# Loading stored operands of an fp32 transformer trunk into the tile of their low part, with no staging buffer between

## The chip, the cores and the metric

The kernel runs on one core of one Trainium2 chip, in one launch. The metric is the time of the whole program on the device, in microseconds (us).

## The reference

The program is a trunk of two layers over 1,024 tokens of width 1,024, in float32. Layer 0 mixes tokens by forgetting attention (FoX, 8 heads), layer 1 by chunkwise retention (4 heads); each is followed by a SwiGLU FFN of inner width 2,816, and a last RMSNorm ends it.

```python
def swiglu(h, w_in, w_out):
    gu = h @ w_in
    return (jax.nn.silu(gu[..., :D_FF]) * gu[..., D_FF:]) @ w_out

def reference(x, ...):
    for i in range(DEPTH):
        h = rmsnorm(x, norm_mix[i])
        j = i // N_MIXERS
        if i % N_MIXERS == 0:
            x = x + forgetting_attention(h, fox_w_in[j], fox_b_f[j], fox_w_out[j])
        else:
            x = x + retention(h, ret_w_in[j], ret_w_out[j])
        h = rmsnorm(x, norm_ffn[i])
        x = x + swiglu(h, ffn_w_in[i], ffn_w_out[i])
    return rmsnorm(x, final_norm)
```

Retention projects q, k, v and a gate g from the normed input, rotates q and k, sums `(q k) v` under a decay of the head, norms the result over 512 values of a head, multiplies by `silu(g)` and projects back.

## The kernel before

**High and low parts.** Every float32 operand of a product is split in two fp32r tiles of 128x512: `hi` is the value rounded (a copy by ScalarE, line 98), `lo` is the rest (a subtraction by VectorE, line 99). A product is three matmuls: `hi.hi`, `hi.lo`, `lo.hi`. A pair of such tiles is made by `units(pool)`; the pools are `bpa` with 32 tiles and `bpb` with 24. Weights have their own pool `wp` with tags `wh` and `wl`, 6 tiles each.

**Products.** The large projections (`Products`, lines 617 to 656) multiply blocks of two by two in seven products rather than eight. Each of the seven takes one weight block (A11, S1, S2, A12, S3, A22, S4) and one operand (B11, T1, T2, B21, T3, T4, B22); an operand is four pairs of tiles, one for each of four row blocks. `open` makes the first product, `middle` the next four, `close` the last two. `in_turn` and `paired_out` run many of these one after another, and open the next before they close the current one, except at the end of `in_turn` and, in `paired_out`, for the last of the four column blocks (`n == 3`). Copies by ScalarE free a PSUM bank for the next product: line 666, 683 or 687 behind S3, line 642 behind A11.

**What is kept in memory.** The FFN's inner activations do not fit on the chip. 16 of the 22 blocks are written to memory as the seven operands of two groups (`Stored.put`, tensors `ac0_0_...` to `ac1_1_...`, shown in the profile as ac_T and ac_B) and read back by `Stored.get` when a product of `paired_out` first wants them; the other six are written as they are (`ad`) and read back by `load_units`. In retention the rotated q and k (`qd`, `kd`), the values (`vd`), the gates (`gd`) and the normed results (`zd`) go through memory too. `prepare(h)` brings in one head: `load_k` (k, split, and also transposed by TensorE and scaled into tiles at lines 1034 and 1035), `load_units` for q, `load_v` for the values. `scores(h, ...)` makes `q k` for the next stage while `weighted` multiplies the values in the current one; `state(h)` sums `k v` for the second half of a head.

**Staging.** All of these reads, and the weights of both kinds of projection (`Blocks`, `wtile2`), first land in tiles of tag `st`, 128x1024, of which there are five. A tile of `st` is free again when the splits that read it are done. The half-megabyte loads of `Stored.get` and `load_units` are issued by SP.

**Order.** The order of each engine's instructions is set when the program is built, by a scheduler that goes by the order of the code and by its own estimate of what is ready. On the chip each engine then works its list in order, and waits where something is not there yet.

Of the kernel before, what the change touches and what calls it, by code (L numbers as in the profile page):

```python
# [10 lines left out]
F32 = mybir.dt.float32  # L11
F32R = mybir.dt.float32r
AF = mybir.ActivationFunctionType
ALU = mybir.AluOpType
# [3 lines left out]
P = 128  # L18
# [3 lines left out]
H = 512  # L22
# [15 lines left out]
def trunk(ctx, tc, nc, d, out):  # L38
# [16 lines left out]
    def nm(s):  # L55
        cnt[0] += 1
        return f"{s}_{cnt[0]}"
# [18 lines left out]
    def units(pool):  # L76
        return [pool.tile([P, H], F32R, tag="b", name=nm("b")) for _ in range(2)]
# [19 lines left out]
    def split(hi, lo, src):  # L97
        nc.scalar.copy(hi, src)  # L98
        return nc.vector.tensor_tensor(lo, src, hi.bitcast(F32), op=ALU.subtract)  # L99
# [10 lines left out]
    HALF = (slice(0, H), slice(H, S))  # L110
# [74 lines left out]
    with ExitStack() as fs:  # L185
# [52 lines left out]
        def v_pair(p, rc):  # L238
            ws = []
            wid = VF0 if p == 0 else 256  # L240
            src = d["fox_v0"] if p == 0 else d["fox_v"][p - 1]
            for k in range(0, KT, 2):
                hi, lo = wload(src[:, k * wid:(k + 2) * wid], 2 * wid)
                ws += [(hi[:, j * wid:(j + 1) * wid], lo[:, j * wid:(j + 1) * wid]) for j in range(2)]
            vs = []
            z = small([P, TB, FOX_HEADS], "fz", 1) if p == 0 else None
            for b in range(TB):
                if p == 0 and b in (3, 4):
                    ps = mp.tile([P, H], F32, tag="st", name=nm("mm"), bufs=2)
                else:  # L250
                    ps = mm_fox()
                tk = slice(b % 4 * P, (b % 4 + 1) * P)
                for k in range(KT):
                    xh, xl = xg[k][b // 4]
                    wh, wl = ws[k]
                    nc.tensor.matmul(ps[:, :wid], xh[:, tk], wh, start=(k == 0), stop=False)  # L256
                    nc.tensor.matmul(ps[:, :wid], xh[:, tk], wl, start=False, stop=False)  # L257
                    nc.tensor.matmul(ps[:, :wid], xl[:, tk], wh, start=False, stop=(k == KT - 1))  # L258
                vh = fp.tile([P, 256], F32R, tag="vh", name=nm("vh"), bufs=12)
                vl = fp.tile([P, 256], F32R, tag="vl", name=nm("vl"), bufs=12)  # L260
                r = rc[:, b:b + 1]
                nc.scalar.activation(vh, ps[:, :256], AF.Copy, scale=r)
                nc.vector.scalar_tensor_tensor(vl, ps[:, :256], r, vh.bitcast(F32), op0=ALU.mult, op1=ALU.subtract)
                if p == 0:
                    nc.vector.scalar_tensor_tensor(z[:, b, :], ps[:, 256:VF0], r, bf, op0=ALU.mult, op1=ALU.add)
                vs.append((vh, vl))
            return vs, z
# [150 lines left out]
        for h in range(2):  # L418
            ks.append([fp.tile([P, S], F32R, tag=t, name=nm(t)) for t in ("kh", "kl")])
            for b in range(2):  # L420
                tag, n = (("mm", 3), ("mm", 3), ("st", 2), ("st", 2))[2 * h + b]
# [20 lines left out]
        vs, z = v_pair(0, rc)  # L442
# [22 lines left out]
        for i, (n, b) in enumerate(TILES):  # L465
            if i < 3:
                mm_u(ops[n, b], wo[n][6:], last_o[:1], b, first=False, last=(i < EVAC))
            else:
                if n == len(wo):
                    wo.append(wtile(d["fox_o"][n][:, :7 * P], 7))  # L470
                tag, bufs = TAGS[i]
# [12 lines left out]
    bpb = ctx.enter_context(tc.tile_pool(name="bpb", bufs=24))  # L484
    yq = ctx.enter_context(tc.tile_pool(name="yq", bufs=4))
    sp = ctx.enter_context(tc.tile_pool(name="sp", bufs=1))
# [4 lines left out]
    def bsplit(pool, src):  # L491
        hi, lo = units(pool)
        split(hi, lo, src)
        return hi, lo


    NAMES = ("B11", "T2", "T1", "T3", "B21", "B22", "T4")
    MAP1 = dict(zip(NAMES, (bpb, bpb, bpb, bpa, bpa, bpa, bpa)))
# [3 lines left out]
    class Combos:  # L502
# [32 lines left out]
        def get(self, n):  # L535
            return self.t[n]

    class Stored:
# [15 lines left out]

        def get(self, n):
            if n not in self.t:
                self.t[n] = []
                for i in range(2):
                    st = sp.tile([P, 1024], F32, tag="st", name=nm("st"), bufs=5)
                    nc.sync.dma_start(st, self.d[n][:, i * 1024:(i + 1) * 1024])  # L560
                    self.t[n] += [bsplit(self.pools[n], st[:, HALF[j]]) for j in range(2)]
            return self.t[n]

    def wsplit(src):
# [213 lines left out]

    def load_units(pool, src, gate=None):

        r = []
        st = sp.tile([P, 1024], F32, tag="st", name=nm("st"), bufs=5)
        nc.sync.dma_start(st, src)
        if gate is not None:
            gt = sp.tile([P, 1024], F32, tag="st", name=nm("st"), bufs=5)
            nc.sync.dma_start(gt, gate)
            nc.vector.tensor_tensor(st, st, gt, op=ALU.mult)
        for h in range(2):
            r.append(bsplit(pool, st[:, HALF[h]]))
        return r  # L790

    def out_proj(wsrc, y, acts, xnew, gi, nextw, pools):
# [21 lines left out]
    def ffn(i, X, nrm, xold, xnew, last, nw, pools):  # L814
# [26 lines left out]
        y = paired_out(d["ffn_out_pairs"][i], stored, True, xold)  # L841
        wsrc = d["ffn_out"][i]
        acts = [load_units(bpa if last else bpb, t) for t in ad]
        if not last:
            return out_proj(wsrc, y, acts, xnew, 2, d["ret_qk"][1], MAP2)
# [157 lines left out]
    nc.sync.dma_start(mask, d["ret_mask"])  # L1003

    def load_v(h, b):
        st = sp.tile([P, 1024], F32, tag="st", name=nm("st"), bufs=5)[:, :512]
        nc.sync.dma_start(st, vd[b][:, h * 512:(h + 1) * 512])
        m = vmean[h][:, b:b + 1]
        hi, lo = units(bpb)
        nc.scalar.activation(hi, st, AF.Identity, bias=m)  # L1010
        nc.vector.scalar_tensor_tensor(lo, st, m, hi.bitcast(F32), op0=ALU.add, op1=ALU.subtract)
        return hi, lo
# [46 lines left out]
    def prepare(h):  # L1059
        kk, kt = load_k(h)  # L1060
        qq = [load_units(bpa, qd[h][e]) for e in range(2)]
        vv = [load_v(h, b) for b in range(TB)]
        heads[h] = [kk, kt, qq, vv, None, []]
# [102 lines left out]
    zg = list(zip(zd, [None] * (4 * 1) + gd[4 * 1:]))  # L1166
    y = [[None, None] for _ in range(KT)]
    acts = [load_units(bpa, *t) for t in zg[:8]]
    for n in range(KT):
        w = wtile2(d["ret_o"][n], 8)  # L1170
# [103 lines left out]
```

## Time and profile before

| | us |
|---|---|
| median of 3 runs | 2590.07 (2589.15 to 2590.61) |
| time of the profiled execution | 2592.81 |
| its span, first to last instruction | 2591.0 |
| TensorE busy (matmuls) | 2562.7 (99%) |
| VectorE busy | 1838.6 (71%) |
| ScalarE busy | 1229.5 (47%) |

The profile is of one execution. An engine's busy time is the time in which it had an instruction under way; matmuls overlap at their ends, so a busy TensorE is not one at its peak. The mean granted TensorE clock of the execution is 0.997 of full speed, and DMA moved 312 MB, 120 GB/s over the span.

The first FFN runs from about 520 to 1130 us of the span, retention's heads from about 1580 to 1785 us, the second FFN from about 1940 us to the end.

### The profile page before, as it was taken

What the parts mean: (1) busy time and instruction counts of PE and PEld (TensorE: products, weight loads), DVE (VectorE), ACT (ScalarE), POOL (GpSimd) and SP (SyncE); (2) the same over time, 40 slices, a digit from 0 to 9 for tenths busy, and PEclk for the clock granted to TensorE, in tenths of its full rate; (3) what the DMA queues carried; (4) which work ended last, traced back from release to release, by engine and by line L of the source; (5) the groups of instructions that cost most, each with busy time, mean ns of one, the idle gap of its engine ahead of it and who ended that gap; (6) DMA issues with size and microseconds to landing.
All of it is one profiled execution on the core that took longest, in us unless ns stands there. A gap on an engine that the chain in (4) does not pass through costs nothing.

```text
span 2591.0 us, 35137 instructions
## 1 busy us (share of the span) xinstructions
PE 2562.7 (99%) x12808; PEld 2184.6 (84%) x12808; DVE 1838.6 (71%) x3131; ACT 1229.5 (47%) x2320; POOL 169.5 (7%) x147
## 2 busy tenths in 40 slices
PE   9999999999999999999999999999999999999998
PEld 8889887888888888889898989898888888888788
DVE  6798888866666768886656576885567666667784
ACT  6566666543333454554343435762354333335543
POOL 0143323000000000001001010000000000000000
PEclk9999999999999999999999999999999999999999
DMA  3111142432332345533332334555522332325441
GB/s 131 44 58 65 51 146 96 149 106 95 113 106 98 127 147 182 161 115 124 102 107 98 122 103 154 191 194 195 195 87 94 105 107 94 110 89 179 167 147 66
DMA packets 137695, 312.12 MB, mean 120 GB/s; under 512 B 15665, under 2 KB 28721, under 8 KB 137521
## 3 DMA queue, kind: packets, MB, share of 16 engines
q1 hardware_dynamic: 136800, 309.33, 35.4%
q8 instruction: 100, 1.64, 0.3%
q14 instruction: 75, 0.61, 0.1%
q10 hardware_dynamic: 720, 0.55, 0.1%
HBM read 217.54 MB, written 92.27 MB: 120 GB/s over the span
## 4 chain that ended last, share of the span: by engine, by line
PE 93%; DVE 2%; issue 1%; DMA 1%; ACT 1%; POOL 0%; DVEq 0%; SPq 0%; POOLq 0%; ACTq 0%
PE mm L635 18%; PE mm L636 18%; PE mm L637 18%; PE mm L106 7%; PE mm L107 7%; PE mm L108 7%; PE mm L751 2%; PE mm L749 2%; PE mm L750 2%; PE mm L256 1%; PE mm L257 1%; PE mm L258 1%; DMA st<-ac_T 1%; PE mm L1101 1%; PE mm L1102 1%
## 5 line engine op out<-in xcount | busy, mean ns | idle before, releaser
L635 PE MATMUL mm<-b,wh 128*128 128x512 f32 x2128 | 827.6, 390 | 5.3 <-ACT 22_4491_22622 L683 3.5
L636 PE MATMUL mm<-b,wh 128*128 128x512 f32 x2128 | 829.3, 390 | 0.0
L637 PE MATMUL mm<-b,wl 128*128 128x512 f32 x2128 | 825.9, 390 | 0.0
L98 ACT CAST wh<-st 128x512 fp32r<-128x512 f32 (+1 forms) x449 | 276.4, 617 | 521.7 <-PE mm L636 318.6
L635 PEld LDWEIGHTS mm<-b,wh 128*128 128x128 f32 x2128 | 400.0, 188 | 88.6 <-ACT 22_4491_22622 L683 4.0
L637 PEld LDWEIGHTS mm<-b,wl 128*128 128x128 f32 x2128 | 400.0, 188 | 83.1
L636 PEld LDWEIGHTS mm<-b,wh 128*128 128x128 f32 x2128 | 400.1, 188 | 82.0
L99 DVE TENSOR_TENSOR wl<-st,wh 128x512 fp32r<-128x512 f32 (+1 forms) x449 | 317.7, 711 | 189.6 <-ACT wh L98 186.1
L98 ACT CAST wh<-s 128x512 fp32r<-128x512 f32 x252 | 156.5, 622 | 306.9 <-PE mm L636 272.9
L106 PE MATMUL mm<-b,wh 128*128 128x512 f32 x736 | 286.5, 392 | 7.7 <-ACT b L126 5.4
L107 PE MATMUL mm<-b,wh 128*128 128x512 f32 x736 | 287.4, 391 | 1.7 <-DVE b L99 1.7
L108 PE MATMUL mm<-b,wl 128*128 128x512 f32 x736 | 287.5, 391 | 0.0
L99 DVE TENSOR_TENSOR wl<-s,wh 128x512 fp32r<-128x512 f32 x252 | 179.8, 715 | 93.3 <-ACT wh L98 89.2
L106 PEld LDWEIGHTS mm<-b,wh 128*128 128x128 f32 x736 | 138.7, 189 | 37.1 <-ACT b L126 6.1
L107 PEld LDWEIGHTS mm<-b,wh 128*128 128x128 f32 x736 | 138.7, 188 | 29.5 <-DVE b L99 2.2
L99 DVE TENSOR_TENSOR b<-st,b 128x512 fp32r<-128x512 f32 x216 | 140.7, 675 | 31.4 <-ACT b L98 28.9
L98 ACT CAST b<-st 128x512 fp32r<-128x512 f32 x216 | 124.5, 611 | 80.9 <-DMA st<-ac_T 26.5
L108 PEld LDWEIGHTS mm<-b,wl 128*128 128x128 f32 x736 | 138.7, 188 | 28.1
L750 PE MATMUL mm<-wl,b 128*128 128x256 f32 x448 | 126.6, 283 | 0.0
L749 PE MATMUL mm<-wh,b 128*128 128x256 f32 x448 | 126.3, 283 | 0.0
L751 PE MATMUL mm<-wh,b 128*128 128x256 f32 x448 | 126.3, 283 | 0.0
L588 DVE TENSOR_TENSOR s<-st 128x512 f32<-128x512 f32 x84 | 58.3, 694 | 65.8 <-DMA st<-ffn_in 27.8
(498 smaller groups left out, 3891.2 us busy)
## 6 DMA issues: line engine op xcount, KB each, us to landing
st<-ffn_in SPq DMA_DIRECT2D x88, 512.0 KB, 3.5
st<-ffn_out_pairs SPq DMA_DIRECT2D x32, 512.0 KB, 4.1
st<-ac_T SPq DMA_DIRECT2D x32, 512.0 KB, 4.8
ac_T<-t SPq DMA_DIRECT2D x48, 256.0 KB, 2.4
st<-ac_B SPq DMA_DIRECT2D x24, 512.0 KB, 4.0
st<-fox_qk SPq DMA_DIRECT2D x32, 256.0 KB, 2.7
xo<-xd SPq DMA_DIRECT2D x32, 256.0 KB, 3.0
ac_B<-t SPq DMA_DIRECT2D x32, 256.0 KB, 2.4
```

The costliest lines, as they stand in the source:

```text
L98: nc.scalar.copy(hi, src)
L99: return nc.vector.tensor_tensor(lo, src, hi.bitcast(F32), op=ALU.subtract)
L106: nc.tensor.matmul(ps, wh, xh, start=(first and k == 0), stop=False)
L107: nc.tensor.matmul(ps, wh, xl, start=False, stop=False)
L108: nc.tensor.matmul(ps, wl, xh, start=False, stop=(last and k == n - 1))
L588: nc.vector.tensor_tensor(self.s1, self.a21, self.a22, op=ALU.add)
L635: nc.tensor.matmul(ps, hi[:, js], th, start=first and j == 0, stop=False, skip_group_check=True)
L636: nc.tensor.matmul(ps, hi[:, js], tl, start=False, stop=False, skip_group_check=True)
L637: nc.tensor.matmul(ps, lo[:, js], th, start=False, stop=(j == 3), skip_group_check=True)
L749: nc.tensor.matmul(o, th[:, tk], hi[:, js], start=f, stop=False, skip_group_check=True)
L750: nc.tensor.matmul(o, th[:, tk], lo[:, js], start=False, stop=False, skip_group_check=True)
L751: nc.tensor.matmul(o, tl[:, tk], hi[:, js], start=False, stop=(j == 3), skip_group_check=True)
```

## The change

`landed(pool, src)` is new: it takes a pair of tiles from the pool, has the DMA write the float32 data straight into the `lo` tile, and splits it there, so that `lo` is both source and destination of the subtraction. `Stored.get` uses it with four loads of a quarter-megabyte in place of two of half a megabyte; `load_units` uses it when there is no gate, with two loads in place of one. With a gate, the gate is still loaded into an `st` tile, the operand lands in `lo`, the product is written over the gate, and is split from there. `load_v` also lands in `lo`. `load_k`, the weights and the first loads of attention are as before, and `st` still has five tiles.

```diff
+    def landed(pool, src):
+
+        hi, lo = units(pool)
+        nc.sync.dma_start(lo.bitcast(F32), src)
+        split(hi, lo, lo.bitcast(F32))
+        return hi, lo
+
@@ Stored
         def get(self, n):
             if n not in self.t:
-                self.t[n] = []
-                for i in range(2):
-                    st = sp.tile([P, 1024], F32, tag="st", name=nm("st"), bufs=5)
-                    nc.sync.dma_start(st, self.d[n][:, i * 1024:(i + 1) * 1024])
-                    self.t[n] += [bsplit(self.pools[n], st[:, HALF[j]]) for j in range(2)]
+                self.t[n] = [landed(self.pools[n], self.d[n][:, j * H:(j + 1) * H]) for j in range(4)]
             return self.t[n]
@@ load_units
+        if gate is None:
+            return [landed(pool, src[:, HALF[h]]) for h in range(2)]
         r = []
-        st = sp.tile([P, 1024], F32, tag="st", name=nm("st"), bufs=5)
-        nc.sync.dma_start(st, src)
-        if gate is not None:
-            gt = sp.tile([P, 1024], F32, tag="st", name=nm("st"), bufs=5)
-            nc.sync.dma_start(gt, gate)
-            nc.vector.tensor_tensor(st, st, gt, op=ALU.mult)
+        gt = sp.tile([P, 1024], F32, tag="st", name=nm("st"), bufs=5)
+        nc.sync.dma_start(gt, gate)
         for h in range(2):
-            r.append(bsplit(pool, st[:, HALF[h]]))
+            hi, lo = units(pool)
+            z = gt[:, HALF[h]]
+            nc.sync.dma_start(lo.bitcast(F32), src[:, HALF[h]])
+            nc.vector.tensor_tensor(z, lo.bitcast(F32), z, op=ALU.mult)
+            split(hi, lo, z)
+            r.append((hi, lo))
         return r
@@ load_v
-        st = sp.tile([P, 1024], F32, tag="st", name=nm("st"), bufs=5)[:, :512]
+        hi, lo = units(bpb)
+        st = lo.bitcast(F32)
         nc.sync.dma_start(st, vd[b][:, h * 512:(h + 1) * 512])
         m = vmean[h][:, b:b + 1]
-        hi, lo = units(bpb)
         nc.scalar.activation(hi, st, AF.Identity, bias=m)
         nc.vector.scalar_tensor_tensor(lo, st, m, hi.bitcast(F32), op0=ALU.add, op1=ALU.subtract)
```

## Rows read from the trace of the kernel before

**Rows 1.** The page: each engine's busy time (with its share of the span and its instructions), and the chain that ended last, by engine.

```profile
PE 2562.7 (99%) x12808; PEld 2184.6 (84%) x12808; DVE 1838.6 (71%) x3131; ACT 1229.5 (47%) x2320; POOL 169.5 (7%) x147
...
PE 93%; DVE 2%; issue 1%; DMA 1%; ACT 1%; POOL 0%; DVEq 0%; SPq 0%; POOLq 0%; ACTq 0%
```

**Rows 2.** The waits of TensorE's matmuls in five stretches, in order of time (0 to 600, 600 to 1200, 1200 to 1700, 1700 to 2100, 2100 to the end): who waited for whom, us in total, times, the longest; the longest of the first, all of the second and third (the fourth has none), and of the last the two that are in the FFN.

```profile
PE mm L106 <- ACT b L126: 5.4, 1, 5.4
...
PE mm L635 <- ACT t L687: 1.4, 1, 1.4
...
PE mm L1029 <- DVE wl L1090: 1.5, 1, 1.5
PE mm L1101 <- DVE wl L1090: 0.3, 1, 0.3
PE mm L1074 <- DVE yv L1131: 0.2, 1, 0.2
...
PE mm L635 <- ACT 22_4491_22622 L683: 3.5, 1, 3.5
...
PE mm L635 <- ACT u L666: 0.4, 1, 0.4
```

**Rows 3.** Windows of 10 us of the first FFN (the one that begins at 1000) and of the second (2420 to 2440): busy time of each engine with its count of instructions, granted TensorE clock, DMA share, GB/s.

```profile
1000.00:1010.00 10.00, 8.63 (x38) 6.82 (x37) 9.25 (x16) 4.92 (x9) 0.00 (x0) 1.00 0.63 202
...
2420.00:2430.00 10.00, 6.46 (x29) 5.04 (x27) 7.98 (x13) 6.24 (x13) 0.00 (x0) 0.99 0.64 206
2430.00:2440.00 10.00, 10.00 (x38) 8.14 (x39) 7.00 (x12) 5.53 (x11) 0.00 (x0) 0.84 0.48 170
```

**Rows 4.** The timeline of TensorE in the second FFN: two matmuls of line 635 that stand three apart (start, us, what).

```profile
2324.81 0.39 PE L635 MATMUL mm<-b,wh 128*128 128x512 f32 x1
...
2325.49 0.39 PE L635 MATMUL mm<-b,wh 128*128 128x512 f32 x1
```

**Rows 5.** The chain that ended last, 2404 to 2430 us, in order of time (start, us, what): its three loads.

```profile
2404.90 4.26 DMA st<-ac_B
...
2411.75 5.74 DMA st<-ac_T
...
2423.30 4.79 DMA st<-ac_T
```

**Rows 6.** ScalarE's timeline in the same place (start, us, what, and in brackets the idle time before it with what ended it).

```profile
2424.73 1.14 ACT L98 CAST b<-st 128x512 fp32r<-128x512 f32 x2 [1.46 <-DMA st<-ac_B]
2428.17 0.62 ACT L98 CAST b<-st 128x512 fp32r<-128x512 f32 x1 [2.30 <-DMA st<-ac_T]
...
2429.21 0.58 ACT L683 COPY 22_4491_22622<-mm 128x512 f32<-128x512 f32 x1
```

**Rows 7.** The waits of ScalarE for loads, over the whole span (us in total, times, the longest).

```profile
ACT b L98 <- DMA st<-ac_T: 26.5, 20, 3.3
...
ACT b L1010 <- DMA st<-vd: 20.5, 13, 4.8
ACT b L98 <- DMA st<-ac_B: 20.5, 17, 2.2
```

**Rows 8.** Groups of instructions by line and shape, 1580 to 1835 us (busy us, mean ns of one, idle time before): the split on VectorE, a sum in place (line 1126), and the multiplication by the gate.

```profile
L99 DVE TENSOR_TENSOR b<-st,b 128x512 fp32r<-128x512 f32 x60 | 39.6, 683 | 3.1 <-ACT b L98 3.0
...
L1126 DVE TENSOR_TENSOR yacc<-yacc,sq 128x512 f32<-128x512 f32 x24 | 16.5, 686 | 1.6 <-ACT sq L1125 1.4
...
L787 DVE TENSOR_TENSOR st<-st,st 128x1024 f32<-128x1024 f32 x12 | 14.7, 1222 | 6.1 <-DMA st<-gd 6.0
```

**Rows 9.** The issues of line 560 on SP: ns of one issue (min, median, max), first and last start.

```profile
L560 SPq DMA_DIRECT2D st<-ac_T x32: 319/320/327, 887.8 to 2435.9; - x32
```

**Rows 10.** The DMA issues: number, KB of each, median us from issue to landing.

```profile
st<-vd SPq DMA_DIRECT2D x32, 256.0 KB, 3.3
...
st<-ad SPq DMA_DIRECT2D x12, 512.0 KB, 3.5
...
st<-qd SPq DMA_DIRECT2D x8, 512.0 KB, 6.1
```

**Rows 11.** Windows of the first FFN, 910 to 930 us, where the operands of its first group are read (columns as in rows 3).

```profile
910.00:920.00 10.00, 10.00 (x46) 8.29 (x45) 8.79 (x15) 6.19 (x12) 0.00 (x0) 1.00 0.78 268
920.00:930.00 10.00, 10.00 (x46) 8.29 (x45) 9.02 (x15) 6.94 (x13) 0.00 (x0) 1.00 0.66 214
```

**Rows 12.** Timelines of SP, ScalarE and TensorE in retention, by head. Head 1: q's load, the last of the transposed k, q's split, the first scores. Head 2: the same without the load.

```profile
1603.04 1.84 SPq L783 DMA_DIRECT2D st<-qd  x2
...
1627.72 0.45 ACT L1034 ACTIVATE b<-mm,kap 128x256 fp32r<-128x256 f32 x1
1628.07 1.13 ACT L98 CAST b<-st 128x512 fp32r<-128x512 f32 x2
...
1632.08 0.48 PE L1074 MATMUL mm<-b,b 128*128 128x512 f32 x1
...
1664.55 0.85 ACT L1034 ACTIVATE b<-mm,kap 128x256 fp32r<-128x256 f32 x2
...
1666.41 0.63 ACT L98 CAST b<-st 128x512 fp32r<-128x512 f32 x1
...
1671.00 0.40 PE L1074 MATMUL mm<-b,b 128*128 128x512 f32 x1
```

## Prediction

> **What bounds the kernel now.** I read the page first. TensorE is busy 99% of the span and the chain that ended last runs through it for 93% [rows 1]. So a change to loads can give back only what TensorE loses by waiting, and the next view is its waits, stretch by stretch [rows 2]. They are few: 5.4 us at the start, before anything the diff touches, and then only short ones. Three stretches hold reloads of the kind that the diff moves. In the first FFN there is one wait of 1.4 us, for the copy of line 687. In retention there are 1.5, 0.3 and 0.2 us. In the second FFN there are 3.5 us, for the copy of line 683, and 0.4 us, for line 666.
>
> What they cost is read from the windows, since the clock may fall behind an idle stretch [rows 3]. A full window of 10 us counts 46 matmuls, as in [rows 11]. The window with the 1.4 us wait counts 38, so 8 x 0.227 = 1.8 us are lost; the step of 0.227 us is that of the rows of one product, three matmuls in 0.68 us [rows 4]. The two windows around the 3.5 us wait count 29 and 38 against 92, so 25 x 0.227 = 5.7 us: the granted clock, 2.4 GHz elsewhere, has a mean of 0.84 in the second of them, that is, it was at its lower level (1.2 GHz) for 3.2 of 10 us. The window with the 1.4 us wait stays at 1.00. Together: 5.7 + 1.8 + 0.4 + 2.0 = **9.9 us** are all that is lost in the stretches that the diff changes, 0.38% of the span.
>
> Why the copies come late is read from the chain and from ScalarE's own rows [rows 5, 6]. Before the 3.5 us wait the chain goes through three loads of stored operands, of 4.26, 5.74 and 4.79 us, one behind another with splits between them: a load waits for a staging buffer, the buffer for a split, the split for a load. ScalarE takes its work in order: it stands 1.46 us and 2.30 us before two splits whose loads are late, and the copy that frees the PSUM bank (2429.21) is queued behind them. Over the run ScalarE stood 26.5 and 20.5 us for stored operands and 20.5 us for values of retention [rows 7]; nearly all of that was hidden.
>
> **The change part by part.**
>
> *Splits.* Their number is the same: 0.62 us on ScalarE [rows 6] and 683 ns on VectorE for a 128x512 half. The subtraction is now made in place; the in-place sum of line 1126, of the same shape, takes 686 ns, so the difference is 3 ns and I take zero [rows 8].
>
> *More and smaller DMAs.* Stored operands 56 to 112, FFN tails 12 to 24, q 8 to 16, ungated z 4 to 8, gated z 12 pairs to 12 triples; values stay at 32. That is 92 issues more, at 0.32 us each [rows 9] 29 us on SP, which has nothing else to do and waits for buffers most of the time. Bound: 0 to 0.32 us where a weight load is queued directly behind. I take zero.
>
> *Gated z.* One multiplication of 1.222 us becomes two of half the width, 0.686 us each by the in-place row [rows 8]: 0.15 us more, 12 times, 1.8 us of VectorE under work in which TensorE never waited. Zero on the path; 1.8 us if that cover is gone.
>
> *Stored operands, no staging.* The load now waits for TensorE to release the unit, not for a staging buffer. Each product uses an operand for 12 matmuls, 2.7 us; an operand's units are released in one product and its successor is wanted six or seven runs later, so 16 to 19 us. In that time a quarter-megabyte must land (3.3 us by loads of that size, 6.1 us by the slowest group [rows 10]) and be split (1.3 us): 4.6 to 7.4 us, hidden. The bytes do not change: 28 quarters (7.3 MB) and the weights of two products (2.1 MB) go in 16 runs, 43.5 us, 216 GB/s, and before it moved 268 and 214 GB/s there [rows 11]. What goes away is the chain of a load waiting for a split waiting for a load; the five staging buffers then serve weights alone, which can only be earlier. What stays is that ScalarE works in order and that at the end of a group no product stands between the third sum's product and the one that needs its bank. The 1.4 us wait in the first FFN is at such a place, the end of its second group; I take its price as what remains of the long one, at the end of the first group of the second FFN: 5.7 - 1.8 = **3.9 us gained**. Bounds: 7.9 us gained (all three FFN waits gone), and nothing gained.
>
> *Values.* Their units come from pool bpb, where nothing else is queued in retention, so half a head's values can be loaded a stage early. The waits of ScalarE for them (up to 4.8 us [rows 7]) should go, and with them up to **2.0 us** of TensorE.
>
> *Queries.* Here a new wait is added. The traces show units of a pool taken in the order of the program: q's splits come right behind the line-1034 activations that take the transposed k's units (1627.72 then 1628.07; 1664.55 then 1666.41), though q of head 1 had been issued to staging at 1603.04, 25.0 us ahead [rows 12]. Once q lands in its own units, its load can only be issued where its split stood. The first scores then stood 4.0 and 4.6 us behind the first split (1632.08, 1671.00), and they now stand behind a landing as well, 3.3 us by the median of the loads of values. What is queued behind: on ScalarE the score evacuations, on TensorE scores of the next head; TensorE can meanwhile run weighted products and the state of the next head. Head 0 is covered, since its q is brought in while projections still run. For heads 1 to 3: from nothing each (weighted products cover 3.3 us) to 6.1 us each (the slowest group of loads, no cover). TensorE's waits in this stage so far were 1.5, 0.3 and 0.2, on average 0.7 us, though operands came up to 4.8 us late; I take that, 3 x 0.7 = **2.0 us lost**.
>
> Sum: -3.9 - 2.0 + 2.0 = **-3.9 us**. The profiled execution took 2592.81 us for a span of 2591.0; the median of the runs is 2590.07, 2.7 below it, and a difference carries over: **2586.2 us**, 0.15% less. Measurement tells about 0.2% (5.2 us) from no change, so I call this the same.
>
> **The rivals.**
>
> *All of it goes.* With no chain of staging all 9.9 us come back and q is covered: 2580.2 us. For it: the longest wait has three late loads in its chain, and values came late in retention. Against it: q's wait, and the 1.4 us in the first FFN, which may be ScalarE's own queue. It counts as faster from 5.2 of the 9.9 us.
>
> *The new wait for q decides.* If TensorE stands 4.8 us (the longest wait for a load in this stage) for each of heads 1 to 3, that is 14.4 lost against 5.9 gained: +8.5, **2598.6 us**, slower. It decides from (5.2 + 5.9) / 3 = 3.7 us a head. For it: the next head's scores stand ahead of weighted products in program order, so they are put just where q was expected. Against: 20 us of ScalarE waiting in this stage cost TensorE 2.0.
>
> *Loads in a burst.* Unthrottled quarters are issued as units come free, and ScalarE stands before splits whose data is late at each change to a stored group, two in each FFN: 4 x 5.7 = 22.8 against the 7.9 lost in the FFNs before: +14.9, with values and q as above 2605 us. Against it: 16 us of slack, and DMA engines at 0.66 to 0.78 before [rows 11]. The Trainium skill, page "DMA: Bandwidth & Descriptors", section "Rules for kernel authors", asks for transfers of 1 MiB or more; by the fit in its section "Anatomy of one DMA — SWDGE (gpsimd) path", which is for another path than SP's, a quarter would take an estimated 2.6 us and a half 3.2, so two quarters in turn 2.0 us longer than one half. The profile shows quarters landing in 3.3 and halves in 3.5 to 6.1 us [rows 10]; the rule speaks for this rival, whose time stands without it.
>
> *The staging didn't matter.* The long wait is ScalarE's order, not the staging, and comes back elsewhere: 2590 us.
>
> **How the numbers follow.** Forecast 0.36, all of it 0.27, q 0.16, burst 0.06, no effect 0.15. The forecast's own range, 2582 to 2590, reaches a little over the line for faster (2584.9): of its 0.36 I give 0.05 to faster; of q's 0.16 0.02 to same. Faster 0.32, same 0.48, slower 0.20. The range of 8 in 10 runs from 2579.5 (all of it, with a little beyond) to 2598.5 (q at its price): outside are the burst, 0.06, half of q beyond its price, 0.08, and 0.05 below.
>
> **What would show it.** Right: no wait for line 683 of 3 us in the second FFN and the clock at its upper level there; no staging load of stored operands; ScalarE's waits for values gone; q issued only behind the line-1034 activations, with TensorE waits at the next head's scores below 1 us each. Wrong: a wait of TensorE at line 1074 or 1075 of over 3.7 us a head, or new waits of 3 us or more at products of the FFNs with a lower clock behind them (slower); or none left at all in these stretches (faster).

## The result, and the profile after

The changed kernel takes 2601.93 us (median; 2595.70 to 2604.66), the kernel before it 2590.03 us on the same chip: a ratio of 1.0044, with a 95% interval of 1.0033 to 1.0055. It is slower by 11.4 us ((ratio - 1) x 2590), outside the range of the prediction and on the other side of no change. Its runs spread over 9.0 us, those of the kernel before over 4.0. The profiled execution took 2600.76 us for a span of 2598.9 us, 7.9 us more than the span before.

The page of the kernel after answers [rows 1]: each engine's busy time, and the chain that ended last.

```profile
PE 2567.0 (99%) x12808; PEld 2184.1 (84%) x12808; DVE 1840.8 (71%) x3143; ACT 1229.2 (47%) x2320; POOL 170.3 (7%) x147
...
PE 89%; DMA 3%; DVE 3%; issue 2%; ACT 1%; SPq 0%; POOL 0%; POOLq 0%; DVEq 0%; ACTq 0%
```

TensorE is still the bound, but its share of the chain has gone from 93% to 89% and that of the transfers from 1% to 3%. Both kernels stream the same matmuls in the same number, so the span can be cut at the same matmuls (counted by the columns streamed), and the time between two cuts compared. Microseconds more than before, one profiled execution of each kernel, so a difference of 1 or 2 us can be scatter; a column adds up to the difference of the spans. e1 is explained below.

```
stretch of before           after     e1
0 to 860                    +0.59   +0.12
860 to 1046, first FFN      +1.39   +2.91
1046 to 1565                 0.00    0.00
1565 to 1757, heads         +8.79   -0.21
1757 to 1910, z             +1.63    0.00
1910 to 2300                 0.00    0.00
2300 to 2400, second FFN    +1.17   -0.69
2400 to 2540, second FFN    -4.91   -5.15
2540 to the end             -0.76   -0.25
```

So the gain came where it was forecast, and the loss sits in the heads of retention, with something in z. The waits of TensorE answer [rows 2]; line numbers are three to six higher in this kernel, so 638 is 635 of before, 686 is 683 and 1106 is 1100. Stretches 600 to 1200, 1560 to 1760, 1760 to 2100 and 2100 to the end:

```profile
PE mm L638 <- ACT b L98: 1.6, 2, 1.1
...
PE mm L1106 <- ACT wh L1095: 2.4, 1, 2.4
PE mm L1106 <- DVE b L99: 2.0, 1, 2.0
PE mm L1107 <- DVE wl L1096: 1.1, 1, 1.1
...
PE mm L106 <- ACT b L98: 0.8, 1, 0.8
...
PE mm L638 <- ACT u L669: 1.5, 1, 1.5
...
PE mm L638 <- ACT 22_4387_22602 L686: 0.2, 1, 0.2
```

The 3.5 us for line 683 have become 0.2 us for line 686. New are 2.4, 2.0 and 1.1 us before the weighted products of the heads (lines 1106 and 1107), which wait for evacuations and splits of score blocks (lines 1095 and 1096) and, the 2.0 us, for the split of the state out of its PSUM bank (line 99). The windows show what stands around them (columns as in [rows 3]):

```profile
1610.00:1620.00 10.00, 7.22 (x30) 5.25 (x29) 8.01 (x19) 7.72 (x18) 0.00 (x0) 0.83 0.45 133
...
1650.00:1660.00 10.00, 6.75 (x30) 4.87 (x29) 10.00 (x20) 5.64 (x15) 0.00 (x0) 0.95 0.50 157
1660.00:1670.00 10.00, 10.00 (x60) 9.28 (x60) 6.71 (x28) 3.33 (x10) 0.00 (x0) 0.88 0.23 63
...
2420.00:2430.00 10.00, 10.00 (x46) 8.29 (x45) 8.01 (x13) 5.62 (x11) 0.00 (x0) 1.00 0.55 177
2430.00:2440.00 10.00, 9.87 (x44) 7.85 (x42) 6.91 (x12) 7.58 (x15) 0.00 (x0) 1.00 0.80 256
```

In the second FFN 90 matmuls of 92 stand where [rows 3] had 67, at 1.00 of the clock. In the heads the granted clock has a mean of 0.83 behind the gap of 2.4 us at 1611.9, that is, it was at 1.2 GHz for 0.17 / 0.5 of the 10 us, 3.4 us, and 0.95 and 0.88 in the window of the other two gaps and the one behind it, another 1.0 + 2.4 us. That is 6.8 us at the lower level, 3.4 us lost. TensorE's waits in the heads add up to 6.2 us, against 2.0 before [rows 2]: 4.2 + 3.4 = 7.6 of the 8.8 us.

Why the score blocks are late is told by the three queues around the values of head 0. SyncE issues their loads, ScalarE splits them (line 1016), TensorE wants the scores. Timelines of SP, ScalarE and TensorE (idle time before an instruction in brackets):

```profile
1599.84 0.38 SPq L1014 DMA_DIRECT2D b<-vd  x1
...
1602.11 0.38 SPq L1014 DMA_DIRECT2D b<-vd  x1
1605.07 0.32 SPq L972 DMA_DIRECT2D gd<-o  x1
1605.48 0.88 SPq L1014 DMA_DIRECT2D b<-vd  x2
```

```profile
1603.80 0.72 ACT L1016 ACTIVATE b<-b,vmean 128x512 fp32r<-128x512 f32 x1 [2.13 <-DMA b<-vd]
1604.42 0.61 ACT L971 ACTIVATE o<-o 128x512 f32<-128x512 f32 x1
1607.02 0.72 ACT L1016 ACTIVATE b<-b,vmean 128x512 fp32r<-128x512 f32 x1 [1.98 <-DMA b<-vd]
1610.01 0.72 ACT L1016 ACTIVATE b<-b,vmean 128x512 fp32r<-128x512 f32 x1 [2.26 <-DMA b<-vd]
...
1613.68 0.58 ACT L1095 ACTIVATE wh<-mm,kap 128x384 fp32r<-128x384 f32 x1
```

```profile
1611.53 0.39 PE L1082 MATMUL mm<-b,b 128*128 128x512 f32 x1
1614.31 0.92 PE L1106 MATMUL mm<-wh,b 128*128 128x512 f32 x2 [2.39 <-ACT wh L1095]
```

ScalarE stands three times for a value, 6.4 us together, and reaches the evacuation of line 1095 at 1613.68; TensorE has finished the scores by 1611.9 and stands 2.39 us until that evacuation is done. The three queues also hold each other up. The load of 1605.48 us goes out right behind a store of the gates (line 972), for which SP stood 2.5 us; that store waited for ScalarE's activation of 1604.42 (line 971), which was queued behind the split that had waited for the load of 1599.84 us. A late value so delays the load of a later one.

A head later it is a query. The chain that ended last, around q of head 1 (start, us, what):

```profile
1630.86 2.06 SPq L1147
...
1634.39 5.74 DMA b<-qd
```

The load of q is issued 0.6 us after the last activation of the transposed k (line 1040) has begun and behind four issues of gate loads (line 1147) on SP, and ScalarE stands 5.86 us until it has landed. Further ahead in SP's queue stood value loads that waited for units, the last until 1626.73:

```profile
1633.77 0.51 ACT L1040 ACTIVATE b<-mm,kap 128x256 fp32r<-128x256 f32 x1
1640.15 0.62 ACT L98 CAST b<-b 128x512 fp32r<-128x512 f32 x1 [5.86 <-DMA b<-qd]
```

### The profile page after: what moved, and what is told of

Its sections match the earlier page's. It is cut to its first block, busy times and chain, and to the rows that moved or that the text cites. A ratio compares the mean times of both kernels' runs of the same rounds, so it can differ in the third digit from the quotient of the medians.

```text
span 2598.9 us, 35315 instructions
## 1 busy us (share of the span) xinstructions
PE 2567.0 (99%) x12808; PEld 2184.1 (84%) x12808; DVE 1840.8 (71%) x3143; ACT 1229.2 (47%) x2320; POOL 170.3 (7%) x147
## 4 chain that ended last, share of the span: by engine, by line
PE 89%; DMA 3%; DVE 3%; issue 2%; ACT 1%; SPq 0%; POOL 0%; POOLq 0%; DVEq 0%; ACTq 0%
PE mm L638 18%; PE mm L639 18%; PE mm L640 18%; PE mm L107 6%; PE mm L106 6%; PE mm L108 6%; PE mm L754 2%; PE mm L752 2%; PE mm L753 2%; DMA b<-ac_T 1%; PE mm L256 1%; PE mm L257 1%; PE mm L258 1%; DMA b<-zd 1%; PE mm L1107 1%
## 5 line engine op out<-in xcount | busy, mean ns | idle before, releaser
L98 ACT CAST b<-b 128x512 fp32r<-128x512 f32 x160 | 97.6, 620 | 115.4 <-DMA b<-ac_B 40.2
L99 DVE TENSOR_TENSOR b<-b,b 128x512 fp32r<-128x512 f32 x160 | 107.6, 686 | 53.9 <-ACT b L98 53.3
```

## Experiments

Which of the parts costs is asked by e1 to e4 and e6. Why it costs was told in four ways, which the other kernels were made to tell apart: the loads of other things that now run ahead crowd the DMA (e7, theory D); the load can't be issued before the operand's unit is free (e8 and e10, theory U); ScalarE's order lets finished scores wait behind a late load (e5, e9, theory H); it is the landing itself, now behind the release of the unit (e11, e12, theory L). Every kernel is made from the kernel after. Ratios are to the kernel before, on the same chip; microseconds in round brackets are (ratio - 1) x 2590.

**e1: the feed-forward halves alone.** The old helper, under the name `staged_units`, and the old `load_v` serve q, z and the values again; the stored groups and the tails of both FFNs stay landed.

```diff
-        hi, lo = units(bpb)
-        st = lo.bitcast(F32)
+        st = sp.tile([P, 1024], F32, tag="st", name=nm("st"), bufs=5)[:, :512]
...
-        qq = [load_units(bpa, qd[h][e]) for e in range(2)]
+        qq = [staged_units(bpa, qd[h][e]) for e in range(2)]
...
-    acts = [load_units(bpa, *t) for t in zg[:8]]
+    acts = [staged_units(bpa, *t) for t in zg[:8]]
```

> Only the FFNs' reloads land in their own units (stored operands and the six FFN tails); q, values and z are staged as before. In the traces, compared at equal numbers of matmul columns done, the changed kernel is 1.4 us behind in the first FFN, 8.8 us in retention's heads, 1.6 us at z, and 3.7 us ahead in the second FFN. Theory A (these are the shares of the parts): 1.4 - 3.7 = -2.3, so about 2587.7 us, not to be told from before. Theory B (the FFN part loses in most executions, and the profiled one is a lucky one): over 2594 us.

Measured: 2587.54 us, ratio 0.9991 [0.9981, 1.0000] (-2.3 us). The heads and z are back at -0.21 and 0.00 us in the table above. So the stored operands gave, within the interval, what the prediction had put on them, and everything that was lost comes from q, the values and z.

**e2, e3, e4: after, with one of the three staged again.** q in e2 and the values in e3, by the lines of e1's diff; in e4 all of z, by the same lines.

> The changed kernel with q alone staged as before. Theory Q (retention loses because q's load is queued behind the transposed k's units, and ScalarE stands 5.9 us before its split): most of the 8.8 us come back, 2594 to 2596 us. Theory V (it loses because the values now wait for their units and land late, ScalarE standing 2.1, 2.0 and 2.3 us before them in head 0): 2600 us or more, as with the whole change.

> The changed kernel with the values alone staged as before. Theory Q: 2600 us or more. Theory V: 2594 to 2597 us. If each has a part, both this run and the one with q staged lie between, near 2598.

> The kernel after, with z and its gates staged as before; the queries, the values and the two feed-forward halves stay landed. Theory A (stages independent; the profiled executions put +0.9 to +2.1 us into z's stage wherever z is landed and 0.0 where it is staged): 2601.9 - 1.6 = 2600.3, ratio 1.0036. Rival (z's loads and gates fight with the heads' loads for DMA and staging buffers, since the gates now come alone into the buffers): staging z takes back several us of the heads too, under 2598. Second rival (z's stage pays what the heads' late end left over): no change, 2602.

Measured: e2 2596.59 us, 1.0023 [1.0013, 1.0032] (+6.0 us); e3 2593.89 us, 1.0010 [1.0001, 1.0019] (+2.6); e4 2596.81 us, 1.0027 [1.0017, 1.0037] (+7.0). Beside e1 (-2.3) and after (+11.4) each price can be read twice. Taken out of the full change, q was worth 11.4 - 6.0 = 5.4 us, the values 8.8, z 4.4. From the three pairs on top of e1 (values and z +8.3, q and z +4.9, q and values +9.3): q 2.9, values 6.4, z 2.0. The intervals leave some 4 us on each difference, so only this is clear, that the values cost the most; z by itself is at the edge of what can be told. The two readings differ because the parts don't add up: 18.6 us by the first, 11.3 by the second, 13.7 lost. The profiled executions say the same: the heads' stretch, +8.8 us in after, is +3.9 in e2, +2.0 in e3 and +9.5 in e4, and that of z, +1.6 in after, is 0.0 in e4. Against the expectations, e2 and e3 each gave back part, and more than the third case said; e4 came under the rival's 2598 us, but its profiled execution doesn't show the rival's gain in the heads.

**e5: q brought in ahead of k.** The load of q then doesn't stand behind the units of the transposed k.

```diff
-        kk, kt = load_k(h)
         qq = [load_units(bpa, qd[h][e]) for e in range(2)]
+        kk, kt = load_k(h)
```

> The changed kernel with one change of order: in prepare(h), q is brought in ahead of k, so that its units are taken before those of the transposed k. Theory Q: the load starts early, ScalarE no longer stands before it, 2594 to 2596 us, like q staged. If it is not the place in the queue that costs but the landing as such, 2600 us or more.

Measured: 2598.08 us, 1.0039 [1.0026, 1.0052] (+10.1 us). ScalarE's waits for q fell from 14.5 us to 11.1, and TensorE now stood 1.0 to 1.9 us at the transposes of k. The time lies between the two expectations and can't be told from after's; the place in the program moved the wait rather than took it away.

**e6: the second FFN alone.** As e1, and the first FFN staged as well.

```diff
+            self.first = name.startswith("ac0")
...
+                if self.first:
...
+                else:
                     self.t[n] = [landed(self.pools[n], self.d[n][:, j * H:(j + 1) * H]) for j in range(4)]
```

> Only the second feed-forward half keeps the change (its stored groups and its last eight gated activations); the first one, the queries, the values and z are staged as before. The kernel with both halves landed came to 2587.5 us, 3.5 less than the kernel before, and its one profiled execution put +2.9 us into the first half and -5.8 us into the second (-0.7 up to 2400 us, -5.1 behind it). Theory A, the stages are independent and the first half's loss is real: 2591.0 - 5.8 = about 2585, ratio 0.9977 (2584 to 2587). Rival, the first half's +2.9 us is the scatter of one execution, or is a shift that the later stages take back: 2587 to 2588, as with both.

Measured: 2587.26 us, 0.9989 [0.9980, 0.9998] (-2.8 us), the same as e1. The first FFN's +2.9 us in e1's profiled execution is within the scatter: this kernel, in which that half is not changed, shows +0.65 there and others -1.7 to +2.1. The gain is the second half's, as far as these intervals tell.

**e7: no run-ahead.** In after, k of the later heads and the gates of z are loaded early into the staging buffers that q and the values no longer use, at the same time as the loads that the heads stand for. Here k of a head is put behind the values of the head before on SP's queue, and z's first eight loads, with their gates, behind the last values.

```diff
-        nc.sync.dma_start(st, vd[b][:, h * 512:(h + 1) * 512])
+        lastv[h] = nc.sync.dma_start(st, vd[b][:, h * 512:(h + 1) * 512]).ins
...
-            nc.sync.dma_start(st, kd[h][e])
+            with tc.issue_after(lastv[h - 1]) if h else nullcontext():
+                nc.sync.dma_start(st, kd[h][e])
```

> The kernel after, with an order added on SP's queue: the staged loads of k of head h + 1 are issued behind the last value load of head h, and the first eight of z's loads behind the last value load of head 3. Nothing else is changed. Theory D (the freed staging buffers run ahead: loads of later k and of z's gates share the DMA with the loads that the heads stand and wait for): the waits of ScalarE for q and the values get shorter, q's landing falls from 4.8 to under 4 us, and the heads lose 3 us or less instead of 8.8: 2594 to 2597. Theory U (each load waits for its own operand's buffer and is issued too late, whatever else the DMA carries): the waits stay, 2600 to 2603; more, if k itself now comes late.

Measured: 2599.72 us, 1.0039 [1.0025, 1.0053] (+10.1 us). Heads +6.8 us in place of +8.8, z +4.6 in place of +1.6. ScalarE still stood 20.8 us for values (20.3 in after) and 10.9 for q. So the run-ahead is not what costs most.

**e8: staging in the two places where ScalarE stood.** Values of head 0 and queries of heads 1 to 3 staged, the rest landed.

```diff
+        if h == 0:
+            st = sp.tile([P, 1024], F32, tag="st", name=nm("st"), bufs=5)[:, :512]
+        else:
...
-        qq = [load_units(bpa, qd[h][e]) for e in range(2)]
+        qq = [(staged_units if h else load_units)(bpa, qd[h][e]) for e in range(2)]
```

> The kernel after, with the values of head 0 and the queries of heads 1 to 3 staged again: the two places where the trace of after shows ScalarE standing before a load and TensorE idle behind it (three stands of 2.0 to 2.3 us at 1604 to 1610 us, one of 5.9 us at 1634 us). The values of heads 1 to 3, the queries of head 0 and all of z stay landed. Theory U (the loss sits where a load can only be issued once its operand's buffer is free, and these are the places): the 8.8 us of the heads go to about 1, and what is left is the two feed-forward halves' -3.5 and z's +1.6: 2589 to 2591. Rival (every landed load of the heads costs a little, through the DMA or the pool that is bound for longer): the values of heads 1 to 3 keep half of what values cost alone, 2593 to 2596.

Measured: 2598.36 us, 1.0030 [1.0019, 1.0042] (+7.8 us), above both expectations. The loss didn't vanish from those places, it changed its owner. ScalarE's timeline at the old place, with the wait of TensorE and the load in the chain that ended last behind it:

```profile
1614.25 0.72 ACT L1034 ACTIVATE b<-b,vmean 128x512 fp32r<-128x512 f32 x1 [4.84 <-DMA b<-vd]
...
1615.58 0.57 ACT L1113 ACTIVATE wh<-mm,kap 128x384 fp32r<-128x384 f32 x1
```

```profile
PE mm L1124 <- ACT wh L1113: 4.1, 1, 4.1
```

```profile
1606.50 7.72 DMA b<-vd
```

In this kernel's order on ScalarE the split of head 1's first value stands ahead of the score evacuations of head 0, and its load landed 7.72 us after its issue. TensorE waited 4.1 us, more than the 2.4 us in after. So ScalarE met a late load ahead of score evacuations in both orders, in another place.

**e9: the values' splits behind the scores.** If only the order were at fault, putting the waiting work last would mend it.

```diff
     a = [scores(0, 0, dg) for dg in range(4)]
+    split_v(0, last)
+    heads[0][4] = state(heads[0][1], heads[0][3])
...
         a = an
+        if ib == 1 and nxt:
+            split_v(h + 1, last)
```

> The kernel after, with the splits of a head's eight values put, on ScalarE and VectorE, behind the evacuations of that head's first four score blocks. The value loads are issued where they were, into the same operand tiles; only the place of the work that waits for them changes. The runs so far give values landed alone about +6 us, queries +3.4, z +3, both feed-forward halves -3.5. Theory H (ScalarE takes its work in a fixed order and stands before a value that lands late, while finished score blocks wait behind it and TensorE for them): the scores no longer wait, TensorE's gap of 2.4 us at 1614.3 us goes, the heads fall from +8.8 to +3 or +5, and the time to 2595 to 2598. Theory N (TensorE needs the values themselves, and they are late wherever their split stands): no gain, 2600 to 2604, and up to 2608 where the splits, put behind, come late for the state and the weighted sums.

Measured: 2618.83 us, 1.0112 [1.0097, 1.0127] (+29.0 us), far beyond theory N's own mark. The waits of TensorE in the heads:

```profile
PE mm L1061 <- ACT b L1023: 9.7, 4, 3.4
```

Line 1061 is the state, which is made of the values (split in line 1023): it now stood once a head. Here TensorE itself wanted the values before their splits were done. This kernel adds more delay than it takes away, so it shows that putting the splits last doesn't mend the loss; it neither prices theory H nor rules it out.

**e10: one unit more, one staging buffer less.**

```diff
-    bpb = ctx.enter_context(tc.tile_pool(name="bpb", bufs=24))
+    bpb = ctx.enter_context(tc.tile_pool(name="bpb", bufs=26))
...
-            st = sp.tile([P, 1024], F32, tag="st", name=nm("st"), bufs=5)
+            st = sp.tile([P, 1024], F32, tag="st", name=nm("st"), bufs=4)
```

> The kernel after, with one staging buffer less (4 of 1024 columns) and the memory given to the second operand pool (26 tiles of 512 columns for 24: one more unit). Theory U (the loss is the short time between the moment when an operand's tile is free and the moment when its split is due): each value load can be issued one value earlier, some 0.7 to 3 us by the spacing of the value loads (1599.8, 1602.1, 1605.5 us), ScalarE's stands before values of about 2 us nearly vanish, and 2 to 5 of the values' 6 us come back: 2597 to 2600. Rival (staging is what carries the heads: k, z's gates and the weights stand in those buffers, and one less costs what the unit gains): 2601 to 2606.

Measured: 2609.61 us, 1.0084 [1.0067, 1.0101] (+21.8 us; 10.4 more than after). Two things were changed at once (heads +15.5 us, z +5.6): the unit and the lost staging buffer together cost 10.4 us, so the kernel does not bear theory U out, and what each did by itself is not shown.

**e11 and e12: the landing taken away.** The splits read the resident mask tile; the units, the splits and the matmuls stay.

```diff
         hi, lo = units(bpb)
-        st = lo.bitcast(F32)
-        nc.sync.dma_start(st, vd[b][:, h * 512:(h + 1) * 512])
+        st = mask
...
-        qq = [load_units(bpa, qd[h][e]) for e in range(2)]
+        qq = [[bsplit(bpa, mask) for i in range(2)] for e in range(2)]
```

> The kernel after without the 32 value loads: each value's split reads the resident mask tile and writes the same operand tiles in the same places (the values are left out of the computation; matmuls, splits and buffers are those of after). Theory L (what costs is the landing behind the moment when the operand's tile comes free: 3.4 to 4.8 us that a staging buffer used to cover): the values' 6 us come back, 2594 to 2597, and TensorE's gap of 2.4 us at 1614.3 us goes. Rival (the operand tiles themselves come free too late, or the order of ScalarE is changed by the other loads): 2599 to 2602, with ScalarE now standing for matmuls that free the tiles instead of for loads.

> The same, and the 16 loads of queries left out too (their splits read the mask tile as well). What is left of the change is both feed-forward halves (-3.5 us by the kernel that has them alone) and z (+3 by the difference of the kernels with and without it staged). Theory L: the heads' loss is gone, 2588 to 2591; at most 2 us of it stays in the heads' stretch 1565 to 1757 us. Rival: over 2594.

Measured: e11, without the value loads, 2592.77 us, 1.0013 [1.0003, 1.0022] (+3.4 us); e12, without those of q as well, 2590.71 us, 1.0006 [0.9996, 1.0016] (+1.6). More came back in e11 than theory L had put there (2594 to 2597). The heads' stretch goes from +8.8 us to -1.2 and -0.9; that of z stays, +5.8 and +2.9 in these two executions. In e11 the waits of ScalarE in 1590 to 1760 us, those that concern splits:

```profile
ACT b L1015 <- PE mm L1106: 11.5, 8, 3.2
...
ACT b L98 <- DMA b<-qd: 4.3, 3, 2.6
```

TensorE's waits in the heads, and the landing of q (number, KB, median us):

```profile
PE mm L1106 <- DVE wl L1095: 0.8, 1, 0.8
```

```profile
b<-qd SPq DMA_DIRECT2D x16, 256.0 KB, 5.6
```

ScalarE still stands up to 3.2 us until weighted products (line 1106) release a value's unit, and that costs TensorE nothing: its only wait in the heads is 0.8 us. So the late release is harmless by itself. Nor is a landing behind it harmful by itself: q still lands in its own units here, in 5.6 us by the median (4.8 in after), ScalarE stands 4.3 us for it in place of 14.5, and the heads lose nothing; leaving its loads out as well (e12) changes nothing there.

Three things left with the value loads: their landing, their traffic, and the time that SP stands for their units (56.3 us in after, shown in the next section), which holds up every issue behind them, q's too. e7 moved traffic aside and gained 1.3 us of 11.4, less than its interval tells. No kernel here takes away the landing alone or SP's standing alone, so which of the two costs is not shown; what is shown is that the loss of the heads comes with loading the values into their own units and goes without these loads. With z (2.0 to 4.4 us by e2 to e4) and the FFNs (-2.3) the remainder of e12, 1.6 us, is accounted for within its interval.

## Why the prediction was wrong, step by step

**What bounds the kernel.** Right: TensorE, and what it loses by waiting. What was not looked for is what it might come to lose in stretches where it waited for nothing before.

**Splits and gates' arithmetic.** Right: the split in place takes 686 ns (683 before [rows 8]) in 160 instances.

**Stored operands.** Right in sign and place, and in size within the interval: -3.9 us forecast, -2.3 [-4.9, 0.0] measured, in the second FFN, with the clock at its upper level there. One number inside was wrong without harm. I let a quarter land in 3.3 us, by the loads of values, and 6.1 as the bound. Number, KB and median us from issue to landing, in the kernel after:

```profile
b<-ac_T SPq DMA_DIRECT2D x64, 256.0 KB, 5.5
...
b<-ac_B SPq DMA_DIRECT2D x48, 256.0 KB, 4.6
...
b<-vd SPq DMA_DIRECT2D x32, 256.0 KB, 3.8
...
b<-qd SPq DMA_DIRECT2D x16, 256.0 KB, 4.8
```

ScalarE's waits for the stored groups even grew, against 20.5 us for ac_B and 26.5 for ac_T in [rows 7]:

```profile
ACT b L98 <- DMA b<-ac_B: 40.2, 17, 4.4
...
ACT b L98 <- DMA b<-ac_T: 33.7, 18, 4.3
...
ACT b L1016 <- DMA b<-vd: 20.3, 13, 2.9
...
ACT b L98 <- DMA b<-qd: 14.5, 5, 5.9
```

Nearly all of it is hidden, as the 16 to 19 us of cover said. The copy that was late before now stands behind waits of 0.2 and 0.5 us, where it stood behind 1.46 and 2.30 [rows 6]. ScalarE's timeline at the end of the first group of the second FFN:

```profile
2438.38 0.63 ACT L98 CAST b<-b 128x512 fp32r<-128x512 f32 x1 [0.47 <-DMA b<-ac_T]
...
2439.42 0.58 ACT L686 COPY 22_4387_22602<-mm 128x512 f32<-128x512 f32 x1
```

That the missing chain of staging buffers brought this, as the prediction has it, is not shown: the loads took no less from issue to landing, and ScalarE waited longer for them in all.

**Values.** This is the step that failed, in sign. "Their units come from pool bpb, where nothing else is queued in retention, so half a head's values can be loaded a stage early" gave -2.0 us; they cost 6.4 to 8.8. The units are not free: the queue of SP stands until weighted products release them, and it stands for the gates' stores of the last projection too (lines 971 and 972). Waits of SP in 1590 to 1760 us, after:

```profile
SPq L1014 <- PE mm L1108: 38.7, 10, 10.4
...
SPq L1014 <- PE mm L1107: 17.6, 9, 3.5
...
SPq L972 <- ACT o L971: 7.5, 2, 5.0
SPq L972 <- ACT u L971: 6.7, 2, 5.3
```

From 1614 us on 19 of 20 value loads are issued only then, and land 3.8 us later by the median. For head 0 it was SP's queue: the loads at 1602.11 and 1605.48 us show no wait for a unit, but stood behind the gates' stores, which stood for ScalarE; so they came one by one, and ScalarE met each of them late. In before the last four splits of head 0 had their data and ran in one piece, held up only by the matmuls that release the units:

```profile
1600.82 2.77 ACT L1010 ACTIVATE b<-st,vmean 128x512 fp32r<-128x512 f32 x4 [1.68 <-PE mm L636]
```

ScalarE's waits for values, which "should go", stayed at 20.3 us (20.5 in [rows 7]). The step also kept only one end of the range: "up to 2.0 us" gained, with no loss beside it, although no row of before showed a value load waiting for a unit. The landing that was priced for q was due here eight times a head, and a queue of SP that stands was not priced at all.

**Queries.** Right in sign: the load of head 1 is issued where the split stood, behind the activations of the transposed k, and lands 5.74 us later. But SP shows no wait for a unit before the loads of q of heads 1 to 3; what stood ahead of them in its queue were loads of values, k and gates and, in heads 2 and 3, stores of z. The term was mis-sized: +2.0 us forecast, 2.9 to 5.4 measured, and it depends on what else is loaded: with the values' loads left out (e11) q cost the heads nothing, with the values staged (e3) the heads lost 2.0 us. The 0.7 us a head came from waits of TensorE in a kernel where q was never late. The rival with 4.8 us a head, 14.4 in all, was too dear.

**Gated z.** A second step that failed: zero, "under work in which TensorE never waited", for 2.0 to 4.4 us. Only the arithmetic was priced there, not a load that now comes later. The loads of z, ns of one issue, first and last start, before and then after:

```profile
L783 SPq DMA_DIRECT2D st<-zd x16: 319/320/320, 1706.4 to 1822.7; - x16
```

```profile
L792 SPq DMA_DIRECT2D b<-zd x24: 319/407/680, 1732.6 to 1858.0; - x24
```

They begin 26 us later and the last ones run into the products. SP's waits for a unit of z are 0.5 us or less; just before the first of these loads it stood 12.4 us for a store of z (line 1149). The chain that ended last in after, just ahead of TensorE's 0.8 us of waiting at 1858.8:

```profile
1850.87 3.88 DMA b<-zd
...
1858.14 0.63 ACT b L98
```

**DMA issues.** +92 at no price: not tested alone. An issue into a unit took 0.38 to 0.43 us by the median at line 499 and 0.32 at line 1014, for 0.32 in [rows 9].

**The rivals and the range.** The case "q decides" pointed the right way, slower at 2598.6 us, but for a third of the loss: q, values and z together made it. The range ended at 2598.5 because the values and z had no cost at their far end; with the 4.8 us [rows 7] that q was allowed, put on one value of each of four heads (4 x 4.8 = 19.2 us), the range would have held the result. "All of it goes" is out by the result, "the staging didn't matter" by the wait for line 683: the FFNs' waits, 5.3 us before [rows 2], are 3.3 us in after (1.6, 1.5 and 0.2), the longest 1.5 for 3.5, and the second FFN, from 2300 us to the end, is 4.5 us shorter. "Loads in a burst" is out: at its four places, the changes of stored group, TensorE waited at most 1.5 us, not 5.7, and the granted clock stayed at 1.00 behind these waits.

## What to carry to other kernels

A staging buffer is not only a copy: it lets a transfer land while the operand's own tile is still in use. Loading straight into that tile puts the whole landing behind its last reader, so ask for each load how long it is from that reader to the next use: with 16 to 19 us of other products between, in the FFN, it was free and even gained 2.3 us; in retention, where most value loads stood for their units, it cost 6.4 to 8.8 us for values, 2.9 to 5.4 for queries, 2.0 to 4.4 for z. And ask what stands behind such a load in its queue: SP stood 56.3 us for the values' units, and the loads and stores behind them stood too. The change is worth keeping in the FFNs alone (2587.5 us, 0.09% under the kernel before, at the edge of what can be told), and a new wait needs a price for a loss even where the old trace shows no wait.

## What the runs showed of the hardware

Half the bytes did not land sooner among many other transfers: quarters of the stored operands of 256 KB took 5.5 and 4.6 us (median of `ac_T` and `ac_B`), where halves of 512 KB had taken 4.8 and 4.0 us in before:

```profile
st<-ac_T SPq DMA_DIRECT2D x32, 512.0 KB, 4.8
...
st<-ac_B SPq DMA_DIRECT2D x24, 512.0 KB, 4.0
```

The prediction's estimate of 2.6 us for a quarter, by the fit in the Trainium skill, page "DMA: Bandwidth & Descriptors", section "Anatomy of one DMA — SWDGE (gpsimd) path", is not borne out by these loads; they go by SP's queue, for which that fit was not made. A single 256 KB value took 7.72 us in e8.

A gap of TensorE of 2.4 us brought the lower clock with it: in after 3.4 us at 1.2 GHz behind the gap of 2.39 us, so that a wait of 2.4 us cost about 2.4 + 1.7 us. The gaps of 2.0 and 1.1 us at 1656 and 1659.6 us were together followed by as much; behind gaps of 1.1 and 1.5 us in the FFNs the granted clock stayed at 1.00.
